# Half of the gate's columns of a hybrid decoder layer in seven products over all rows, in turn with the plain half

## The chip, the cores and the metric

One core of one Trainium2 chip runs the whole layer in one launch. The metric is the device time in microseconds of that launch; lower is better. TensorE is called PE, VectorE DVE, ScalarE ACT, GpSimd POOL and SyncE SP, as in the profile.

## The reference, cut to what matters

The layer has 256 rows (tokens) of 2048 values. After two token mixers and an MLP, each row passes a gated per-layer embedding, and that last line is what the change touches:

```python
x = x + merged @ w_out[i]
hm = rmsnorm(x, g_mlp[i])
x = x + jnp.square(jax.nn.relu(hm @ w_up[i])) @ w_down[i]
hp = rmsnorm(x, g_ple[i])
x = x + (p[i] @ w_ple_proj[i]) * jax.nn.sigmoid(hp @ w_ple_gate[i])
```

`w_ple_gate` is 2048 x 2048, all values are float32.

## The kernel before

Every product is made in three matmuls on split operands: an operand is cut into a high part (`wh`, a copy by ACT to a type that PE takes at full rate) and a remainder (`wl`, a subtraction by DVE). `split_weights` does that for 128x1024 pieces of a loaded quarter of weights (`raw`, 1 MB, three buffers; `wh` and `wl` have three buffers each). A matmul writes 128 rows by 512 columns into a bank of PSUM; there are eight banks, four under the name `ps_mm` and four under `ps_at`. Each engine works through its own list of instructions in a fixed order and waits in it for semaphores.

The MLP runs in blocks `s` of 1024 hidden columns. `up_units` makes the hidden values, transposed; `hidden` squares them and, for most blocks, also adds four sums of the 128x128 pieces of a pair of row tiles, so that `fast_units` can make a 2x2 product of blocks in seven products in place of eight. `plain_units` makes it in eight. `together` calls such streams in turn by fixed fractions. The row residual is `xr` (two tiles of 128 rows), to which `add_rows` adds.

The block `s = 7` is plain (`last_units`, 16 units), in turn with the embedding `p @ w_ple_proj` (`embedding_units`, into `em`). As column groups of 512 of `xr` are complete, `finished` sums their squares on ACT (`squares_rows`) and sets `turn` a few microseconds later by a clock that is counted in the program: PE transposes `xr` by 128x128 pieces, ACT and DVE split each pair of pieces into `h3`, scaled by the gain. `later(us, ...)` and `advance(us)` are that clock: they decide only where in the order an instruction stands.

The gate then runs over four groups of 512 columns. Each loads four quarters of weights, and 16 slices of 128 of the inner dimension go through three matmuls for each of the two row tiles: 384 matmuls. `gate_out` ends a group: sigmoid by ACT (with the row norm `rms[1]` as scale), product with `em` and addition of `xr` by DVE, and the store from SP. SP also issues all weight loads, in its own order.

Of the kernel before, what the change touches and what calls it, by code (L numbers as in the profile page):

```python
# [59 lines left out]
def layer_kernel(ctx: ExitStack, tc: tile.TileContext, xt, xm, pt, gains, qkg, cst,  # L60
# [15 lines left out]
    def bank(tag):  # L76
        return psum.tile([P, 512], F32, tag=tag, name=f"ps_{tag}")
# [415 lines left out]
    mw = mlp.enter_context(tc.tile_pool(name="mw", bufs=2))  # L493
    FAST = [(s, 0) for s in range(7)]

    def hidden(s, fast):

        n = 8 if fast else 4  # L500
        nc.scalar.activation(s, s, AF.Relu)
        r = mw.tile([P, n, P], F32, tag="hr", name="hr", bufs=1)
        nc.scalar.activation(r[:, 0:4, :].rearrange("p a t -> p (a t)"),
                             s.rearrange("p a t -> p (a t)"), AF.Square)
        if fast:
            a21, a11, a22, a12 = (r[:, i, :] for i in range(4))
            nc.vector.tensor_tensor(r[:, 4, :], a11, a21, op=ALU.subtract)
            nc.vector.tensor_tensor(r[:, 5, :], a21, a22, op=ALU.subtract)
            nc.vector.tensor_tensor(r[:, 6, :], r[:, 5, :], a11, op=ALU.subtract)
            nc.vector.tensor_tensor(r[:, 7, :], r[:, 6, :], a12, op=ALU.add)  # L510
        u = hid.tile([P, 2, n, P], F32R, tag="hid", name="u")
        split(u[:, 0], u[:, 1], r)
        return u
# [162 lines left out]
    ss2 = const.tile([P, 2, 4], F32, name="ss2")  # L676
    h3 = []

    def finished(g):
        if g == 0:  # L680
            h3.extend(new_acts("h3_", pool=blk))
        for tt in range(2):
            squares_rows(tt, g, ss2, mw.tile([P, PIECE], F32, tag="cp", name="junk", bufs=5))
        later(3, turn, g, h3, 2)

    def last_units(u):
        for n in range(2):
            yield from plain_units(7, n, u)
            finished(2 * n)
            finished(2 * n + 1)  # L690

    hids = [[]]
    for _ in up_units(0, hids[0]):
# [11 lines left out]
    later(6, lambda: rms.append(rows_norm(ss2, "rt2", mw)))  # L705


    def gate_out(g, tt, ps, c0, n):

        a, c = g * PIECE + c0, slice(g * PIECE + c0, g * PIECE + c0 + n)  # L710
        o = mw.tile([P, n], F32, tag="cp", name="o", bufs=5)
        nc.scalar.activation(o, ps[:, c0:c0 + n], AF.Sigmoid, scale=rms[1][:, tt:tt + 1])
# [4 lines left out]
    for g in range(4):  # L717
        ps = [bank("mm") if g % 2 else bank("at") for _ in range(2)]
        for c in range(4):
            for i, (wh, wl) in enumerate(weights(wpg[g, c], 4, PIECE)):  # L720
                kt = 4 * c + i
                for tt in range(2):
                    t = slice(tt * P, (tt + 1) * P)
                    nc.tensor.matmul(ps[tt], h3[kt][:, 0, t], wh, start=kt == 0, stop=False)  # L724
                    nc.tensor.matmul(ps[tt], h3[kt][:, 0, t], wl, start=False, stop=False)  # L725
                    nc.tensor.matmul(ps[tt], h3[kt][:, 1, t], wh, start=False, stop=kt == DT - 1)
                advance(1.36)
        for tt in range(2):
            gate_out(g, tt, ps[tt], 0, PIECE)
    mlp.close()  # L730


# [61 lines left out]
```

## Time and profile before

| | us |
|---|---|
| median of 3 runs | 1487.3 (1486.57 to 1488.2) |
| the profiled execution, whole | 1486.83 |
| its span in the trace | 1485.1 |
| last MLP block with the embedding, 1331.30 to 1389.88 | 58.58 |
| gate, 1389.88 to 1479.03 | 89.15 |
| end, 1479.03 to 1485.10 | 6.07 |

The stretches are cut at the first and last matmuls of a part. Matmuls overlap in the trace: each shows from its start to its modelled end, so their cost is read from start to start. The rows the prediction uses stand in a section of their own.

### The profile page before, as it was taken

To read this page: it belongs to the slowest core of one execution; us is meant where nothing else is said; L and a number is where in the kernel's file an instruction comes from. 1 tells how busy PE (TensorE), PEld (TensorE's weight loads), DVE (VectorE), ACT (ScalarE), POOL (GpSimd) and SP (SyncE) were. 2 spreads that over 40 slices of the span, in tenths; PEclk is the share of its full clock that TensorE was granted. 3 is DMA by queue.
4 is the path that set the end of the run, shared out by engine and by line. 5 is a ranking of instruction groups with operands and counts; after the bars stand their busy time and mean duration, and the time that the engine had idled before them with its cause. 6 is when DMAs were issued, how large, how long until landed. Compare 5 with 4: busy or idle time off the path is not lost.

```text
span 1485.1 us, 17838 instructions
## 1 busy us (share of the span) xinstructions
PE 1470.0 (99%) x6960; PEld 1209.4 (81%) x6960; DVE 1002.1 (67%) x1209; ACT 839.2 (57%) x1084; POOL 49.2 (3%) x65
## 2 busy tenths in 40 slices
PE   8999999999999999999999999999999999999998
PEld 6788888888888888888787887878888788888886
DVE  5975555455555555556878879788787878766654
ACT  6545555488834444546655655656565655656543
POOL 0641000000000000000000000000000000000000
PEclk9999999999999999999999999999999999999999
DMA  8555544544455555557455564645546465444563
GB/s 334 197 193 179 172 167 169 174 167 171 171 197 197 173 197 184 185 193 289 142 201 195 175 225 141 227 168 197 200 157 238 144 205 194 154 144 167 206 218 109
DMA packets 40341, 279.09 MB, mean 188 GB/s; under 512 B 4624, under 2 KB 4880, under 8 KB 7104
## 3 DMA queue, kind: packets, MB, share of 16 engines
q1 hardware_dynamic: 39600, 275.01, 53.4%
q0 software_dynamic: 512, 2.92, 0.5%
q8 instruction: 54, 0.88, 0.2%
q14 instruction: 31, 0.25, 0.0%
q10 hardware_dynamic: 144, 0.02, 0.0%
HBM read 275.83 MB, written 2.10 MB: 187 GB/s over the span
## 4 chain that ended last, share of the span: by engine, by line
PE 91%; DVE 4%; issue 2%; ACT 1%; DMA 1%; SPq 0%; DVEq 0%; ACTq 0%
PE ps_mm L525 15%; PE ps_mm L139 13%; PE ps_mm L138 13%; PE ps_mm L137 13%; PE ps_mm L526 8%; PE ps_mm L628 4%; PE ps_mm L629 4%; PE ps_mm L627 3%; PE ps_at L547 3%; PE ps_at L545 2%; PE ps_at L549 2%; DVE wl L83 2%; ACT wh L82 1%; PE ps_at L725 1%; PE ps_at L724 1%
## 5 line engine op out<-in xcount | busy, mean ns | idle before, releaser
L83 DVE TENSOR_TENSOR wl<-raw,wh 128x1024 fp32r<-128x1024 f32 (+1 forms) x462 | 563.9, 1229 | 336.4 <-ACT wh L82 330.6
L82 ACT ACTIVATE wh<-raw 128x1024 fp32r<-128x1024 f32 (+1 forms) x462 | 484.9, 1053 | 388.6 <-PE ps_mm L139 209.4
L525 PE MATMUL ps_mm<-h,wh 128*128 128x512 f32 x1024 | 366.0, 398 | 0.0
L526 PE MATMUL ps_mm<-h,wl 128*128 128x256 f32 x1024 | 287.2, 281 | 0.4
L137 PE MATMUL ps_mm<-wh,h 128*128 128x512 f32 x640 | 254.9, 399 | 2.0 <-ACT wh L82 1.7
L138 PE MATMUL ps_mm<-wl,h 128*128 128x512 f32 x640 | 250.9, 392 | 1.2 <-DVE wl L83 1.1
L139 PE MATMUL ps_mm<-wh,h 128*128 128x512 f32 x640 | 250.8, 392 | 0.0
L525 PEld LDWEIGHTS ps_mm<-h,wh 128*128 128x128 f32 x1024 | 192.3, 188 | 46.2 <-ACT wh L82 2.2
L526 PEld LDWEIGHTS ps_mm<-h,wl 128*128 128x128 f32 x1024 | 193.2, 189 | 8.1 <-DVE wl L83 3.1
L83 DVE TENSOR_TENSOR wl<-quart,wh 128x1024 fp32r<-128x1024 f32 x98 | 120.0, 1224 | 83.7 <-ACT wh L82 83.5
L82 ACT ACTIVATE wh<-quart 128x1024 fp32r<-128x1024 f32 x98 | 104.0, 1061 | 123.4 <-PE ps_mm L525 89.1
L138 PEld LDWEIGHTS ps_mm<-wl,h 128*128 128x128 f32 x640 | 120.9, 189 | 27.9 <-DVE wl L83 3.9
L137 PEld LDWEIGHTS ps_mm<-wh,h 128*128 128x128 f32 x640 | 120.6, 189 | 28.1 <-ACT wh L82 4.4
L139 PEld LDWEIGHTS ps_mm<-wh,h 128*128 128x128 f32 x640 | 120.7, 189 | 25.5
L628 PE MATMUL ps_mm<-wl,u 128*128 128x512 f32 x256 | 101.9, 398 | 4.0 <-DVE wl L83 3.9
L629 PE MATMUL ps_mm<-wh,u 128*128 128x512 f32 x256 | 100.2, 391 | 0.0
L627 PE MATMUL ps_mm<-wh,u 128*128 128x512 f32 x256 | 98.0, 392 | 0.0
L547 PE MATMUL ps_at<-wl,u 128*128 128x512 f32 x196 | 80.4, 410 | 0.0
L545 PE MATMUL ps_at<-wh,u 128*128 128x512 f32 x196 | 78.6, 401 | 0.0
L549 PE MATMUL ps_at<-wh,u 128*128 128x512 f32 x196 | 76.8, 392 | 0.0
L559 DVE TENSOR_TENSOR quart<-quart 128x2048 f32<-128x2048 f32 x28 | 64.0, 2287 | 0.5
L628 PEld LDWEIGHTS ps_mm<-wl,u 128*128 128x128 f32 x256 | 48.1, 188 | 18.3 <-DVE wl L83 9.3
(198 smaller groups left out, 1704.8 us busy)
## 6 DMA issues: line engine op xcount, KB each, us to landing
raw<-in_wa SPq DMA_DIRECT2D x79, 1024.0 KB, 4.8
raw<-in_wup SPq DMA_DIRECT2D x64, 1024.0 KB, 4.8
raw<-in_wdn SPq DMA_DIRECT2D x36, 1024.0 KB, 4.8
quart<-in_wdn SPq DMA_DIRECT2D x28, 1024.0 KB, 4.8
raw<-in_wo SPq DMA_DIRECT2D x16, 1024.0 KB, 4.8
raw<-in_wpg SPq DMA_DIRECT2D x16, 1024.0 KB, 4.8
raw<-in_wba SPq DMA_DIRECT2D x8, 1024.0 KB, 4.8
raw<-in_wbb SPq DMA_DIRECT2D x8, 1024.0 KB, 4.7
```

What stands on the lines that cost most here:

```text
L82: nc.scalar.activation(hi, src, AF.Copy)
L83: nc.vector.tensor_tensor(lo, src, hi.bitcast(F32), op=ALU.subtract)
L137: nc.tensor.matmul(ps[tt], lhs[kt][:, 0, t], wh, start=kt == 0, stop=False)
L138: nc.tensor.matmul(ps[tt], lhs[kt][:, 0, t], wl, start=False, stop=False)
L139: nc.tensor.matmul(ps[tt], lhs[kt][:, 1, t], wh, start=False, stop=kt == last)
L525: nc.tensor.matmul(ps, wh, flat(h2[kt]), start=kt == 0, stop=False)
L526: nc.tensor.matmul(ps[:, :T], wl, h2[kt][:, 0, :], start=False, stop=kt == DT - 1)
L545: nc.tensor.matmul(ps, f[k][:, 0, a, :], wh, start=start and k == 0, stop=False, skip_group_check=not start)
L547: nc.tensor.matmul(ps, f[k][:, 0, a, :], wl, start=False, stop=False, skip_group_check=not start)
L627: nc.tensor.matmul(ps[tt], u[k][:, 0, a, :], wh, start=i + k == 0, stop=False)
L628: nc.tensor.matmul(ps[tt], u[k][:, 0, a, :], wl, start=False, stop=False)
L629: nc.tensor.matmul(ps[tt], u[k][:, 1, a, :], wh, start=False, stop=last)
```

## The change

The left 1024 of the gate's 2048 output columns stay plain (`gate_plain`: two groups of 512, 16 units, 192 matmuls). The right 1024 are computed as a 2x2 product of blocks: rows in two tiles, inner dimension in two halves, columns in two groups of 512. `gate_fast` makes it in seven products of 24 matmuls (14 units, 168 matmuls). Sums of the weights are needed: `chain` is a buffer of two quarters into which further quarters are added by DMAs from POOL (`add_loaded`, 12 transfers of 512 KB); `right` is summed on DVE from two loads. The sums on the side of the rows are made by `four_sums`, so `x` is turned by pairs of tiles: PE transposes, ACT copies with the gain into the buffer `hr` (one buffer), DVE makes four sums, and one split of 128x1024 is written. Six pairs of eight are turned during the last MLP block (groups are now finished one by one), two in the gate. The products' results are kept by ACT and combined by DVE ahead of `gate_out`. Host code orders the weights by `halves`. The core of the diff:

```diff
+    def four_sums(r):
+        a21, a11, a22, a12 = (r[:, i, :] for i in range(4))
+        nc.vector.tensor_tensor(r[:, 4, :], a11, a21, op=ALU.subtract)
+        nc.vector.tensor_tensor(r[:, 5, :], a21, a22, op=ALU.subtract)
+        nc.vector.tensor_tensor(r[:, 6, :], r[:, 5, :], a11, op=ALU.subtract)
+        nc.vector.tensor_tensor(r[:, 7, :], r[:, 6, :], a12, op=ALU.add)
...
+    def turn_pair(k):
+        tp = bank("at")
+        for i in range(2):
+            for tt in range(2):
+                o = (2 * i + tt) * P
+                nc.tensor.transpose(tp[:, o:o + P],
+                                    xr[tt][:, (2 * k + i) * P:(2 * k + i + 1) * P], ident)
+        r = mw.tile([P, 8, P], F32, tag="hr", name="hr", bufs=1)
+        for i in range(2):
+            nc.scalar.activation(r[:, 2 * i:2 * i + 2, :].rearrange("p a t -> p (a t)"),
+                                 tp[:, i * T:(i + 1) * T], AF.Copy,
+                                 scale=gn[:, 2, 2 * k + i:2 * k + i + 1])
+        four_sums(r)
+        u = pair_tile(k)
+        split(u[:, 0], u[:, 1], r)
+        h3.append(u)
...
-        later(3, turn, g, h3, 2)
+        later(3, turn_pair, 2 * g)
+        later(4.5, turn_pair, 2 * g + 1)
...
+    def gate_fast():
...
+        def add_loaded(q, c, i, j):
+            for k in range(0, 4, 2):
+                nc.gpsimd.dma_start(q[:, k:k + 2, :].rearrange("p k c -> p (k c)"),
+                                    wpg[1, i, j, c, :, k * PIECE:(k + 2) * PIECE],
+                                    accum_op=ALU.add)
+
+        def product(ps, a, b, start, then=None):
+            for c in range(2):
+                for p0 in range(2):
+                    parts = split_weights(b(c)[:, 2 * p0:2 * p0 + 2, :], 2, PIECE)
...
+                if then:
+                    add_loaded(b(c), c, *then)
+                if c == 0:
+                    yield
...
+        def finish(tt, j, t, ps, op):
+            nc.vector.tensor_tensor(t, t, ps, op=op)
+            gate_out(tt, (2 + j) * PIECE, t)
...
+        chain = quarter(0, 0, room)
+        px, py = bank("at"), bank("at")
+        yield from product(px, A11, lambda c: chain[c], True, (0, 1))
+        keep_later("x", px)
+        yield
+        yield from product(py, A12, lambda c: load(wpg[1, 1, 0, c], 4, PIECE), True)
+        finish_later(0.6, 1, 0, "x", py, ALU.add)
+        yield
+        pz = bank("at")
+        yield from product(pz, S1, lambda c: chain[c], True, (1, 1))
...
+    together((0.9, 16, gate_plain()), (1.9, 14, gate_fast()))
```

The products follow as A11, A12, S1, S4, S2, S3, A22; `chain` is used by the first, third, fifth and seventh.

What stands in a row on the engines, first ACT at the beginning of the gate, before: `L85` are the copies of the turn, `L82` the high parts of weights and `L214` a step of the row norm. The brackets name the semaphores that an instruction waits for, by engine or DMA queue; numbers behind names are buffers.

```order
L214 ACTIVATE rs_11096<-rv_11094 128x2 [waits DVE_49]
L82 ACTIVATE wh_11084<-raw_11078 128x1024 [waits PE_49,Activation_49]
L85 ACTIVATE h3_2_10766<-ps_at_11036,gn_75 128x256 [waits PE_49]
L85 ACTIVATE h3_2_10766<-ps_at_11045,gn_75 128x256 [waits PE_49]
L85 ACTIVATE h3_2_10766<-ps_at_11036,gn_75 128x256 [waits DVE_49]
L85 ACTIVATE h3_2_10766<-ps_at_11045,gn_75 128x256 [waits DVE_49]
L82 ACTIVATE wh_11125<-raw_11123 128x1024 [waits DMAHW6_49,PE_49,Activation_49]
L85 ACTIVATE h3_3_10767<-ps_at_11054,gn_75 128x256 [waits PE_49]
L85 ACTIVATE h3_3_10767<-ps_at_11063,gn_75 128x256 [waits PE_49]
L85 ACTIVATE h3_3_10767<-ps_at_11054,gn_75 128x256 [waits DVE_49]
L85 ACTIVATE h3_3_10767<-ps_at_11063,gn_75 128x256 [waits DVE_49]
L82 ACTIVATE wh_11129<-raw_11123 128x1024 [waits PE_49,Activation_49]
```

And now, at the same place: `L700` are the copies of a pair into `hr`, `h3u` the split of a pair, `gq` is the weight buffer `chain`.

```order
L214 ACTIVATE rs_11137<-rv_11135 128x2 [waits DVE_49]
L700 ACTIVATE hr_11091<-ps_at_11086,gn_75 128x256 [waits PE_49,Activation_49]
L700 ACTIVATE hr_11091<-ps_at_11086,gn_75 128x256
L82 ACTIVATE h3u_11098<-hr_11091 128x1024 [waits DVE_49,Activation_49]
L700 ACTIVATE hr_11112<-ps_at_11107,gn_75 128x256 [waits DVE_49,PE_49]
L700 ACTIVATE hr_11112<-ps_at_11107,gn_75 128x256
L82 ACTIVATE h3u_11119<-hr_11112 128x1024 [waits DVE_49,Activation_49]
L82 ACTIVATE wh_11128<-gq_11122 128x1024 [waits DMAHW0_49]
L82 ACTIVATE wh_11149<-gq_11122 128x1024
L82 ACTIVATE wh_11163<-raw_11161 128x1024 [waits DMAHW5_49]
L82 ACTIVATE wh_11167<-raw_11161 128x1024 [waits DVE_49,PE_49]
```

The weight splits that stood between the copies of the turn have moved behind both pairs; the first is that of the first fast product.

Next, ACT around the first sigmoid of the gate, before:

```order
L82 ACTIVATE wh_11159<-raw_11157 128x1024 [waits DMAHW7_49,PE_49,Activation_49]
L82 ACTIVATE wh_11163<-raw_11157 128x1024 [waits PE_49,Activation_49]
L82 ACTIVATE wh_11205<-raw_11203 128x1024 [waits DMAHW0_49,DVE_49,PE_49]
L82 ACTIVATE wh_11209<-raw_11203 128x1024 [waits DVE_49,PE_49]
L712 ACT_TABLE_LOAD
L712 ACTIVATE o_11191<-ps_at_11006,rt2_11095 128x512 [waits PE_49]
L712 ACTIVATE o_11196<-ps_at_11007,rt2_11095 128x512 [waits PE_49]
L82 ACTIVATE wh_11239<-raw_11237 128x1024 [waits DMAHW1_49,DVE_49]
L82 ACTIVATE wh_11243<-raw_11237 128x1024 [waits DVE_49,PE_49]
```

And now: `gq` belongs to a fast product, `raw_11330` to the plain half.

```order
L82 ACTIVATE wh_11267<-raw_11265 128x1024 [waits DMAHW5_49,DVE_49,PE_49]
L82 ACTIVATE wh_11279<-raw_11277 128x1024 [waits DMAHW6_49,DVE_49,PE_49]
L82 ACTIVATE wh_11308<-gq_11122 128x1024 [waits DMASW5_49,DVE_49,PE_49]
L82 ACTIVATE wh_11318<-gq_11122 128x1024 [waits DMASW6_49,DVE_49,PE_49]
L743 ACT_TABLE_LOAD
L743 ACTIVATE o_11296<-gk_11211,rt2_11136 128x512 [waits DVE_49]
L82 ACTIVATE wh_11332<-raw_11330 128x1024 [waits DMAHW7_49,PE_49]
L82 ACTIVATE wh_11336<-raw_11330 128x1024 [waits PE_49,Activation_49]
L82 ACTIVATE wh_11352<-gq_11123 128x1024 [waits DMASW7_49,DVE_49,PE_49]
```

The table load and the sigmoid have moved from the border of two plain groups to a place between a fast product's pieces and the plain half's.

Last, the loads on SP at the beginning of the gate, before:

```order
L91 DMA raw_11008<-in_wpg 128x2048 [waits DMAHW2_49,DVE_49]
L91 DMA raw_11078<-in_wpg 128x2048 [waits DMAHW0_49,DVE_49]
L91 DMA raw_11123<-in_wpg 128x2048 [waits DMAHW3_49,DVE_49]
L91 DMA raw_11157<-in_wpg 128x2048 [waits DMAHW4_49,DVE_49]
L91 DMA raw_11203<-in_wpg 128x2048 [waits DMAHW5_49,DVE_49]
L91 DMA raw_11237<-in_wpg 128x2048 [waits DMAHW6_49,DVE_49]
L91 DMA raw_11271<-in_wpg 128x2048 [waits DMAHW7_49,DVE_49]
```

And now: `raw_11219`, `raw_11231`, `raw_11265` and `raw_11277` are the A12 product's.

```order
L91 DMA raw_11058<-in_wpg 128x2048 [waits DMAHW2_49,DVE_49]
L91 DMA raw_11161<-in_wpg 128x2048 [waits DMAHW0_49,DVE_49]
L91 DMA raw_11219<-in_wpg 128x2048 [waits DMAHW3_49,DVE_49]
L91 DMA raw_11231<-in_wpg 128x2048 [waits DMAHW4_49,DVE_49]
L780 DMA gq_11122<-in_wpg 128x2048 [waits PE_49]
L780 DMA gq_11123<-in_wpg 128x2048 [waits PE_49]
L780 DMA gq_11374<-in_wpg 128x2048 [waits PE_49]
L780 DMA gq_11375<-in_wpg 128x2048 [waits PE_49]
L91 DMA raw_11243<-in_wpg 128x2048 [waits DMAHW5_49,DVE_49]
L91 DMA raw_11265<-in_wpg 128x2048 [waits DMAHW6_49,DVE_49]
L91 DMA raw_11277<-in_wpg 128x2048 [waits DMAHW7_49,DVE_49]
L91 DMA raw_11330<-in_wpg 128x2048 [waits DMAHW4_49,DVE_49]
```

Four loads of `chain` and `right` have come in, and the product over A12, whose function of `c` loads, has four.

## Rows read from the trace of the kernel before

**Rows 1.** The page's part 1: busy time, share of the span, instructions.

```profile
PE 1470.0 (99%) x6960; PEld 1209.4 (81%) x6960; DVE 1002.1 (67%) x1209; ACT 839.2 (57%) x1084; POOL 49.2 (3%) x65
```

**Rows 2.** Stretches: length, busy (instructions) of PE, PEld, DVE, ACT, POOL; PEclk, DMA, GB/s.

```profile
1331.30:1389.88 58.58, 58.58 (x269) 48.44 (x267) 35.83 (x41) 35.71 (x54) 0.00 (x0) 1.00 0.54 189
1389.88:1479.03 89.15, 89.15 (x401) 73.46 (x399) 49.73 (x59) 42.18 (x51) 0.00 (x0) 1.00 0.50 171
```

**Rows 3.** Timeline of PE, end of the gate: start, duration, instruction.

```profile
1476.37 0.39 PE L725 MATMUL ps_mm<-wl,h 128*128 128x512 f32 x1
1476.60 0.39 PE L726 MATMUL ps_mm<-wh,h 128*128 128x512 f32 x1
...
1478.64 0.39 PE L726 MATMUL ps_mm<-wh,h 128*128 128x512 f32 x1
```

**Rows 4.** Timeline at a turn of x in the gate: transposes, copies, next matmul.

```profile
1393.97 1.04 PE L465 MATMUL ps_at<-idt,xr 128*128 128x128 f32 x8
...
1394.60 1.94 ACT L85 ACTIVATE h<-ps_at,gn 128x256 fp32r<-128x256 f32 x4 [0.66 <-PE ps_at L465]
...
1394.76 0.47 PE L724 MATMUL ps_at<-wh,h 128*128 128x512 f32 x1
```

**Rows 5.** Timelines of DVE and ACT, an MLP block's sums and split.

```profile
682.92 0.28 DVE L508 TENSOR_TENSOR hr<-hr 128x128 f32<-128x128 f32 x1
...
683.56 0.29 DVE L510 TENSOR_TENSOR hr<-hr 128x128 f32<-128x128 f32 x1
...
683.95 1.06 ACT L82 ACTIVATE u<-hr 128x1024 fp32r<-128x1024 f32 x1
...
685.05 1.22 DVE L83 TENSOR_TENSOR u<-hr,u 128x1024 fp32r<-128x1024 f32 x1
```

**Rows 6.** Groups by line: count, then busy us and mean ns, then idle before.

```profile
L82 ACT ACTIVATE wh<-raw 128x1024 fp32r<-128x1024 f32 x30 | 31.8, 1060 | 37.9 <-PE ps_mm L726 18.5 <-PE ps_at L726 17.8 <-PE ps_at L629 1.7
L83 DVE TENSOR_TENSOR wl<-raw,wh 128x1024 fp32r<-128x1024 f32 x30 | 36.6, 1224 | 31.3 <-ACT wh L82 31.1
L559 DVE TENSOR_TENSOR quart<-quart 128x2048 f32<-128x2048 f32 x28 | 64.0, 2287 | 0.5
L712 ACT ACTIVATE o<-ps_at,rt 128x512 f32<-128x512 f32 x4 | 2.6, 688 | 1.0 <-PE ps_at L726 1.0
L713 DVE TENSOR_TENSOR o<-o,em 128x512 f32<-128x512 f32 x8 | 5.4, 692 | 7.5 <-ACT o L712 7.5
```

**Rows 7.** Timeline of PE at the kernel's start, and one stretch (columns of Rows 2).

```profile
7.68 0.39 PE L139 MATMUL ps_mm<-wh,h 128*128 128x512 f32 x1
9.80 0.73 PE L137 MATMUL ps_mm<-wh,h 128*128 128x512 f32 x2 [1.73 <-ACT wh L82]
10.53 0.64 PE L138 MATMUL ps_mm<-wl,h 128*128 128x512 f32 x1
...
13.96 0.48 PE L138 MATMUL ps_mm<-wl,h 128*128 128x512 f32 x1
...
13.00:14.00 1.00, 1.00 (x4) 0.71 (x4) 1.00 (x3) 1.00 (x3) 0.00 (x0) 0.50 1.00 410
```

**Rows 8.** DMA issues: count, KB each, us to landing; one stretch near the start.

```profile
raw<-in_wpg SPq DMA_DIRECT2D x14, 1024.0 KB, 4.8
...
cs<-in_cst POOLq DMA_DIRECT2D x1, 608.0 KB, 6.6
...
20.00:30.00 10.00, 10.00 (x46) 8.28 (x45) 6.87 (x10) 7.43 (x15) 0.53 (x1) 1.00 1.02 424
```

**Rows 9.** Timeline of ACT at the gate's first sigmoid.

```profile
1412.14 1.28 ACT L712 ACT_TABLE_LOAD   x1
...
1414.60 1.05 ACT L82 ACTIVATE wh<-raw 128x1024 fp32r<-128x1024 f32 x1
```

**Rows 10.** PE's waits over the whole span: us, times, longest.

```profile
PE ps_mm L628 <- DVE wl L83: 3.9, 7, 1.2
```

**Rows 11.** Timeline of DVE, end of the kernel.

```profile
1480.39 1.28 DVE L714 TENSOR_TENSOR o<-o,xr 128x512 f32<-128x512 f32 x2
```

More of the change, by code (lines that the diff above doesn't have):

```diff
@@ L505, in hidden @@
         if fast:
[L506 to L510, printed above, removed]
+            four_sums(r)
         u = hid.tile([P, 2, n, P], F32R, tag="hid", name="u")
@@ L677, in layer_kernel, with pair_tile @@
     h3 = []
+    def pair_tile(k):
+        if k < 4:
+            return block([P, 2, 8, P], F32R, f"h3_{k}", blk)
+        if k < 6:
+            return mw.tile([P, 2, 8, P], F32R, tag="quart", name="h3q", bufs=4)
+        return hid.tile([P, 2, 8, P], F32R, tag="hid", name="h3u")
+    def turn_pair(k):
[10 more added lines that the diff above has]
+                                 scale=gn[:, 2, 2 * k + i:2 * k + i + 1])
+        four_sums(r)
+        u = pair_tile(k)
+        split(u[:, 0], u[:, 1], r)
+        h3.append(u)
     def finished(g):
-        if g == 0:
-            h3.extend(new_acts("h3_", pool=blk))
         for tt in range(2):
             squares_rows(tt, g, ss2, mw.tile([P, PIECE], F32, tag="cp", name="junk", bufs=5))
-        later(3, turn, g, h3, 2)
+        later(3, turn_pair, 2 * g)
+        later(4.5, turn_pair, 2 * g + 1)
     def last_units(u):
         for n in range(2):
-            yield from plain_units(7, n, u)
-            finished(2 * n)
-            finished(2 * n + 1)
+            units = plain_units(7, n, u)
+            for i in range(8):
+                next(units)
+                if i % 4 == 3:
+                    finished(2 * n + i // 4)
+                yield
     hids = [[]]
@@ L705, in layer_kernel, with gate_out @@
     later(6, lambda: rms.append(rows_norm(ss2, "rt2", mw)))
[L708 to L712, printed above, removed]
+    def gate_out(tt, c0, gate):
+        c = slice(c0, c0 + PIECE)
+        o = mw.tile([P, PIECE], F32, tag="cp", name="o", bufs=5)
+        nc.scalar.activation(o, gate, AF.Sigmoid, scale=rms[1][:, tt:tt + 1])
         nc.vector.tensor_tensor(o, o, em[tt][:, c], op=ALU.mult)
@@ L715, in gate_out, with gate_plain @@
         nc.sync.dma_start(out[tt, :, c], o)
[L717 to L721, printed above, removed]
-                for tt in range(2):
[L723 to L729, printed above, removed]
+    def gate_plain():
+        for j in range(2):
+            ps = [bank("mm") for _ in range(2)]
+            for c in range(2):
+                for i in range(2):
+                    raw = load(wpg[0, i, j, c], 4, PIECE)
+                    for k, (wh, wl) in enumerate(split_weights(raw, 4, PIECE)):
+                        for tt in range(2):
+                            a, u = 2 * i + tt, h3[4 * c + k]
+                            last = c == i == 1 and k == 3
+                            nc.tensor.matmul(ps[tt], u[:, 0, a, :], wh, start=c + i + k == 0,
+                                             stop=False)
+                            nc.tensor.matmul(ps[tt], u[:, 0, a, :], wl, start=False, stop=False)
+                            nc.tensor.matmul(ps[tt], u[:, 1, a, :], wh, start=False, stop=last)
+                        advance(1.36)
+                        if k == 1:
+                            yield
+                    if c + i < 2:
+                        yield
+            if j:
+                for tt in range(2):
+                    gate_out(tt, j * PIECE, ps[tt])
+            else:
+                for tt in range(2):
+                    later(0.6 + 1.5 * tt, gate_out, tt, j * PIECE, ps[tt])
+            yield
@@ L751, in quarters, with halves @@
     return np.ascontiguousarray(w).reshape(k // 1024, n // 1024, 2, 2, P, 4 * 512)
+def halves(w):
+    k, n = w.shape
+    w = w.reshape(k // 1024, 4, 2, P, n // 1024, 2, 512).transpose(4, 2, 5, 0, 3, 1, 6)
+    return np.ascontiguousarray(w).reshape(n // 1024, 2, 2, k // 1024, P, 4 * 512)
 def columns(a):
```

59 lines of the change are left out of this document (58 added, 1 removed).

## Prediction

> **What bounds the kernel now.** I read the page first: TensorE is busy for 99% of the span [rows 1], so what a change is worth is the number of matmul slots it saves, less the waits it makes. Then the stretches by time [rows 2]: in the last MLP block (58.58 us) and in the gate (89.15 us) PE is busy throughout at a granted clock of 1.00, while VectorE works 49.73 us of the gate's 89.15 and ScalarE 42.18. The slack on both is what the change spends. Then the order of time inside the gate. A 128x512 matmul shows 0.39 us, but its successor starts 0.23 us later (1476.37 to 1476.60; 1476.37 to the last at 1478.64 is ten steps, 0.227 each) [rows 3]. So one matmul costs 0.227 us of the path, not 0.39.
>
> The profiled execution took 1486.83 us around a span of 1485.1; the median of the runs is 1487.3. The sum below is made against 1486.83.
>
> **The change part by part.**
>
> *Matmuls.* The gate had 4 column groups x 16 x 2 x 3 = 384. Now the plain half has 192 and seven products of 8 x 3 have 168: 360 together, 24 fewer, as the program's order also has it. 24 x 0.227 = **-5.4 us**. The 32 transposes remain; 16 of them stood in the gate, 8 do now, the others move into the MLP block: nothing in the sum (eight cost 0.79 us, 1393.97 to 1394.76 [rows 4]).
>
> *The last two pairs of x.* This is the step that decides. In the old turn, four ScalarE copies and four VectorE subtractions ran side by side: the copies took 1.94 us and PE met no wait [rows 4]. Now one pair is a chain across both engines: two copies, four sums, a split on ScalarE, its remainder on VectorE. All go through one buffer, `hr`, so pair 7 may not copy until pair 6's remainder is written. The ScalarE order shown with the change has nothing between these steps, and behind them stands the first weight split of the first product, which PE needs after 24 gate matmuls.
>
> The chain's length: two copies 0.95 (half of 1.94). From the second sum's start to the last one's end 0.93, then the split 0.10 later, 1.06 long, and the remainder 0.04 after that, 1.22 long: all four steps stand in the trace for an MLP block (682.92 to 683.85, 683.95, 685.05) [rows 5]. With 0.05 at each change of engine, pair 6 takes 0.95 + 0.98 + 0.10 + 1.06 + 0.04 + 1.22 + 0.04 = 4.39. Pair 7 up to its split's end takes 3.09, and the weight split behind it 1.06, less 0.1 where two of an engine's instructions overlap. Sum 8.4. It starts when pair 6's transposes are there: 18 matmuls (4.08) and 0.63 after the transposes began (1393.97 to 1394.60 [rows 4]), at 4.7 us of the gate. So PE gets its first `wh` at 13.1, but is there at 24 x 0.227 + 0.79 = 6.2: it waits 6.9. The low part `wl` follows later, since VectorE finishes pair 7's remainder only at 13.4 and takes 1.22 [rows 6] more: another 1.2. **+8.1 us**. Below: if half of each latency were hidden, 7.5. Queued behind on ScalarE are all further splits, so nothing can run ahead.
>
> *TensorE's clock.* Early in the kernel PE sat idle from 8.07 to 9.80; the granted clock was 0.50 some microseconds later, which is the 1.2 of the two levels 1.2 and 2.4 GHz, and from 10.53 to 13.96 lie eight matmul starts, 0.43 us each [rows 7]. An idle of 6.9 us is longer, so I expect the same once: 3.4 us at half speed cost **+1.7**. Bounds 0 (no fall) and 3. [...]
>
> *Loads.* The A12 product calls for its weight quarter anew for each half of it, so that each quarter is fetched twice: 4 loads, where 2 would do (the SP order shown with the change). The raw pool has three buffers. The second two wait until a buffer is split, and then PE has 6 + 6 + 12 matmuls (5.4 us) less one ScalarE split (1.06) until it needs them: 4.4 us for a load that takes 4.8 [rows 8], while the GpSimd queue adds into SBUF beside it. Two such loads, and each late `wh` brings a late `wl`: **+1.5**, between 0 and 4. The bus moved 424 GB/s when asked [rows 8], and the gate runs at 171 [rows 2]; 24 MB in place of 16 still fit, so only landing times hurt. The Trainium skill (DMA: Bandwidth & Descriptors, section "Issuing engines are not separate DMA queues") says that transfers from all queues interleave on the same engines, so the adds would delay these loads; a landing of 1 MB behind 1 MB of adds would by it be the upper bound rather than the value taken.
>
> *The first sigmoid.* The table load (1.28) and the sigmoids stood ahead of a split that PE did not need at once: the load at 1412.14, the split at 1414.60, and no wait of PE [rows 9]. Now, between two products, ScalarE has a split for a 6-matmul piece, the table load, one sigmoid, and the split of the plain half. Its buffers let it start the first of these only after PE has left the third piece before: 1.06 + 1.28 + 0.69 + 1.06 = 4.1 against 18 matmuls, 4.1. VectorE must do two 0.69 us operations of the output [rows 6] before that split's remainder, so `wl` comes about **+1.2** late; bounds 0 and 1.7.
>
> *The remaining splits.* VectorE's account of the gate: 44 splits x 1.224 + 2 sums x 2.287 + 4 x 0.69 + 16 x 0.69 = 72 us of 82 [rows 6], with two of its instructions per 2.7 us of PE in the fast halves. In the MLP, which is as dense, a plain product sometimes waits for `wl`: 3.9 us in 7 places [rows 10]. I take **+0.8**, between 0 and 2.5. The turns of pairs 2 to 5 now stand before the embedding's `wl` in the MLP block: **+0.6**, between 0 and 1.6.
>
> *The end.* From the last matmul's end (1478.64 + 0.39) to the last addition's (1480.39 + 1.28) were 2.64 us [rows 3, 11]. Now follow an addition out of PSUM, the sigmoid, the product, the addition: 4 x 0.69 + latencies = 2.9, up to 1 us more while the plain half's last four VectorE operations are ahead: **+0.7** (0.3 to 1.4). The last store is the same.
>
> Sum: -5.4 + 8.1 + 1.7 + 1.5 + 1.2 + 0.8 + 0.6 + 0.7 = +9.2; 1486.83 + 9.2 = **1496**. With all terms at their low ends: -5.4 + 7.5 + 0 + 0 + 0 + 0 + 0 + 0.3 = +2.4, 1489; at the high ends -5.4 + 8.1 + 3 + 4 + 1.7 + 2.5 + 1.6 + 1.4 = +16.9, 1504.
>
> **The rivals.**
>
> *The turn is covered (faster).* Place: ScalarE between the first gate split and the first product. If pair 7's copies did not have to wait for pair 6's remainder, or if the first product's split were done ahead of both turns, the 8.1 would shrink; below a wait of about 2 us at that place the clock holds too, and the saving shows: 1486.83 - 5.4 + 0.7 and 0 to 2 for the rest, 1482 to 1484. For it: half of ScalarE's time in the gate is free [rows 2]. Against it: the order on an engine is fixed, and the single `hr` is in it.
>
> *The later waits are repaid (no change).* During the wait, the loads land and ScalarE gets ahead; the clock and the small terms come to nearly nothing, and the stall stays at its low end with them: 1486 to 1490. For it: the small terms are estimates of waits under 2 us. Against it: three split buffers let an engine be ahead by 2 splits only.
>
> *The adds arrive late (much slower).* Twelve transfers of 512 KB add weights onto `chain` in place. Between one use of a half and the next PE has 96 matmuls, 21.8 us; less two splits some 19 us stay for two transfers in a row, so it decides from about 9 us for each. The nearest row, a plain 608 KB transfer of the same queue on a full bus, took 6.6 us [rows 8]; in proportion 5.6. If reading the destination doubles it, 11: 2 x 2 us over, at three reuses, +12, 1508. The Trainium skill (DMA: Bandwidth & Descriptors, section "Rules for kernel authors") says that an accumulating transfer reads its destination and writes it later, which speaks for a doubling; no row here shows one.
>
> That fewer matmuls are not there is ruled out by the order.
>
> **How the numbers follow.** The forecast (1489 to 1504) gets 0.65; the adds late 0.14; covered 0.11; repaid 0.10. The likeliest case's time is 1496. From 1486 to 1508 are left out nearly all of "covered" and the upper half of "late", about 0.18. Both forecast and late adds are slower by over 0.2% (above 1490.3, about what this measurement can tell from no change), save a corner of the forecast that I give to chance: slower 0.78, same 0.11, faster 0.11.
>
> **What would show it.** In the trace of after: one PE wait of 6 to 8 us at the first matmul of the first product, released by ScalarE's `wh`, with ScalarE and VectorE taking turns on `hr` just before; right behind it a granted clock of 0.5 for about 3 us; a wait of one to three microseconds at the second half of A12, with ScalarE waiting for a DMA; matmuls 0.227 apart elsewhere. The prediction is wrong if that first wait is under 3 us, or if ScalarE waits for the GpSimd queue at the second and third use of `chain`.

## The result: 1% slower, and where the 16 us lie

| | us |
|---|---|
| before, 4 runs | 1486.93 (1485.55 to 1488.2) |
| after, 4 runs | 1502.89 (1502.53 to 1503.96) |
| ratio, with its 95% interval | 1.0112 (1.0097 to 1.0127) |
| profiled execution of after, its span | 1503.14, 1501.4 |

The changed kernel is 16 us slower. The forecast was 1496 with a range from 1486 to 1508: the sign and the range hold, the value is 7 us short.

The page of after has the fewer matmuls, 6936 for 6960 in [rows 1], and PE is still busy for 98% of the span. What is new is GpSimd's line, and the landing time of the gate's loads, which was 4.8 us in [rows 8]:

```profile
PE 1472.9 (98%) x6936; PEld 1207.4 (80%) x6936; DVE 1034.0 (69%) x1251; ACT 861.8 (57%) x1108; POOL 59.6 (4%) x77
...
L791 POOL DMA_DIRECT2D gq<-in_wpg x12 | 10.4, 872 | 1342.5 <-DVE wl L83 1342.5
...
raw<-in_wpg SPq DMA_DIRECT2D x14, 1024.0 KB, 6.2
```

The stretch of the gate in after (columns as in [rows 2]): 104.20 us where it was 89.15, and PE stands still for 12.6 of them. The DMA engines went from 0.50 to 0.77:

```profile
1390.90:1495.10 104.20, 91.59 (x369) 70.42 (x367) 73.10 (x81) 56.87 (x65) 10.44 (x12) 0.93 0.77 225
```

PE's timeline in after shows three places (start, duration, instruction, and in brackets the idle time and who ended it):

```profile
1396.82 0.60 PE L696 MATMUL ps_at<-idt,xr 128*128 128x128 f32 x4
1403.96 0.80 PE L802 MATMUL ps_at<-wh,h 128*128 128x512 f32 x1 [6.55 <-ACT wh L82]
1405.41 0.79 PE L804 MATMUL ps_at<-wl,h 128*128 128x512 f32 x1 [0.66 <-DVE wl L83]
...
1423.55 0.39 PE L761 MATMUL ps_mm<-wh,h3q 128*128 128x512 f32 x1
1426.87 0.79 PE L802 MATMUL ps_at<-wh,h3q 128*128 128x512 f32 x1 [2.93 <-ACT wh L82]
1428.13 0.79 PE L804 MATMUL ps_at<-wl,h3q 128*128 128x512 f32 x1 [0.47 <-DVE wl L83]
...
1440.86 0.50 PE L760 MATMUL ps_mm<-wl,h3q 128*128 128x512 f32 x1 [0.91 <-DVE wl L83]
```

The first is the first product, the second the second half of A12, the third the first sigmoid. Behind the first two the granted clock, the third number from the end, falls:

```profile
1400.00:1405.00 5.00, 0.80 (x1) 0.29 (x1) 3.17 (x6) 3.93 (x6) 0.00 (x0) 0.75 0.93 393
1405.00:1410.00 5.00, 4.59 (x12) 3.66 (x13) 3.59 (x4) 1.86 (x2) 1.81 (x2) 0.57 0.56 99
...
1425.00:1430.00 5.00, 2.66 (x5) 1.77 (x6) 2.02 (x2) 2.11 (x2) 0.00 (x0) 0.64 1.01 410
1430.00:1435.00 5.00, 5.00 (x17) 4.00 (x16) 1.65 (x2) 1.06 (x1) 0.86 (x1) 0.68 0.97 360
```

Inside them, in 1406 to 1408 us and in 1429 to 1432, it is 0.50, the lower of its two levels (1.2 and 2.4 GHz), and the matmuls start 0.43 us apart there.

ACT's timeline ahead of the first wait is the chain of the prediction, step by step: copies of pair 6, a wait for the sums, the split, a wait for the remainder of pair 6, the same for pair 7, and only then the first product's `wh` (its two pieces stand as one row):

```profile
1395.68 0.84 ACT L700 ACTIVATE hr<-ps_at,gn 128x256 f32<-128x256 f32 x2 [1.14 <-PE ps_at L696]
1397.59 1.06 ACT L82 ACTIVATE h3u<-hr 128x1024 fp32r<-128x1024 f32 x1 [1.07 <-DVE hr L501]
1400.00 0.84 ACT L700 ACTIVATE hr<-ps_at,gn 128x256 f32<-128x256 f32 x2 [1.35 <-DVE h3u L83]
1401.91 1.06 ACT L82 ACTIVATE h3u<-hr 128x1024 fp32r<-128x1024 f32 x1 [1.07 <-DVE hr L501]
1402.87 1.99 ACT L82 ACTIVATE wh<-gq 128x1024 fp32r<-128x1024 f32 x2
```

The second place is a load. ACT waited 4.88 us for A12's third load; the list of DMA issues of 1416 to 1419 us has that load (1 MB, 9.1 us to landing) and an adding transfer of GpSimd's queue beside it:

```profile
1425.76 1.06 ACT L82 ACTIVATE wh<-raw 128x1024 fp32r<-128x1024 f32 x1 [4.88 <-DMA raw<-in_wpg]
```

```profile
raw<-in_wpg SPq DMA_DIRECT2D x1, 1024.0 KB, 9.1
gq<-in_wpg POOLq DMA_DIRECT2D x1, 512.0 KB, 10.4
```

Start by start, every distance over the usual 0.227 taken together (less what the kernel before has of it), the terms of the prediction come out so:

| term | forecast | measured |
|---|---|---|
| 24 matmuls less | -5.4 | -5.4 (24 x 0.227) |
| first product waits for both turns | +8.1 | 6.7 + 1.2 = +7.9 |
| half clock | +1.7, once | 1.9 + 2.3 = +4.2, twice |
| A12's second half | +1.5 (0 to 4) | 3.1 + 1.0 = +4.1 |
| first sigmoid | +1.2 | 0.5 + 1.2 = +1.7 |
| other late splits (1452.39, 1455.93) | +0.8 | 0.35 + 0.87 = +1.2 |
| turns of pairs 2 to 5 | +0.6 | +0.2 |
| end | +0.7 | 6.70 - 6.46 = +0.2 |
| starts 0.23 to 0.24 apart, most of them in the products | none | about +2.2 |

The sum of the right column is 16.3, and so is the difference of the spans. The turns are read so: the gate begins 1.02 us later than before (1390.90 for 1389.88), and 0.79 of that are the eight transposes that moved into the MLP block, at their price of [rows 4].

### The profile page after: what moved, and what is told of

Read it like the earlier page. It is cut to its first block, busy times and chain, and to the rows that moved or that the text cites. A ratio compares the mean times of both kernels' runs of the same rounds, so it can differ in the third digit from the quotient of the medians.

```text
span 1501.4 us, 17919 instructions
## 1 busy us (share of the span) xinstructions
PE 1472.9 (98%) x6936; PEld 1207.4 (80%) x6936; DVE 1034.0 (69%) x1251; ACT 861.8 (57%) x1108; POOL 59.6 (4%) x77
## 4 chain that ended last, share of the span: by engine, by line
PE 90%; DVE 4%; issue 2%; DMA 2%; ACT 2%; SPq 0%; ACTq 0%; DVEq 0%
PE ps_mm L528 15%; PE ps_mm L139 13%; PE ps_mm L138 13%; PE ps_mm L137 13%; PE ps_mm L529 8%; PE ps_mm L631 4%; PE ps_mm L632 4%; PE ps_mm L630 3%; PE ps_at L550 3%; PE ps_at L548 2%; PE ps_at L552 2%; DVE wl L83 2%; ACT wh L82 1%; DMA raw<-in_wpg 1%; DMA raw<-in_wa 1%
## 5 line engine op out<-in xcount | busy, mean ns | idle before, releaser
L83 DVE TENSOR_TENSOR wl<-raw,wh 128x1024 fp32r<-128x1024 f32 (+1 forms) x454 | 554.1, 1229 | 304.1 <-ACT wh L82 297.7
L82 ACT ACTIVATE wh<-raw 128x1024 fp32r<-128x1024 f32 (+1 forms) x454 | 476.3, 1053 | 359.4 <-PE ps_mm L139 209.2
L82 ACT ACTIVATE wh<-quart 128x1024 fp32r<-128x1024 f32 x98 | 104.0, 1061 | 123.5 <-PE ps_mm L528 89.8
L791 POOL DMA_DIRECT2D gq<-in_wpg x12 | 10.4, 872 | 1342.5 <-DVE wl L83 1342.5
```

The lines of the kernel that those rows point to most:

```text
L82: nc.scalar.activation(hi, src, AF.Copy)
L83: nc.vector.tensor_tensor(lo, src, hi.bitcast(F32), op=ALU.subtract)
```

## Experiments

The theories at this point: **(T)** the first wait is the order on ACT, both turns ahead of the product's first split; **(L)** the second is the doubled load; **(D)** the second is the DMA engines' load, the adds above all. Each run below is compared with the kernel before on the same chip; its median was 1485.8 to 1486.6 there.

| kernel | us | ratio to before (95%) |
|---|---|---|
| turns earlier and apart | 1490.67 | 1.0033 (1.0020 to 1.0046) |
| A12 loaded once | 1500.86 | 1.0099 (1.0084 to 1.0114) |
| no adds | 1494.08 | 1.0055 (1.0040 to 1.0070) |
| own `hr` for pair 7 | 1502.50 | 1.0110 (1.0093 to 1.0127) |
| PE kept busy in both waits | 1500.57 | 1.0096 (1.0081 to 1.0112) |
| new turn, old gate | 1486.70 | 1.0006 (0.9998 to 1.0015) |
| turns apart and A12 loaded once | 1490.81 | 1.0034 (1.0022 to 1.0047) |
| the same, sums by GpSimd | 1493.01 | 1.0042 (1.0030 to 1.0055) |
| plain transfers for the adds | 1498.59 | 1.0078 (1.0063 to 1.0094) |
| turns apart, loaded once, no adds | 1484.24 | 0.9988 (0.9979 to 0.9997) |
| products first, loads earlier | 1485.38 | 0.9995 (0.9986 to 1.0004) |
| the same, a plain piece last | 1484.89 | 0.9990 (0.9981 to 0.9999) |

### The first wait: order, buffer or chain

**The new turn alone**, with the gate of the kernel before. Its product loop only takes its left operand from the pair tiles:

```diff
-                    nc.tensor.matmul(ps[tt], h3[kt][:, 0, t], wh, ...)
+                    u, a = h3[kt // 2], 2 * (kt % 2) + tt
+                    nc.tensor.matmul(ps[tt], u[:, 0, a, :], wh, ...)
```

> The new turn by pairs (two copies, four sums, split and remainder through one hr) with the gate of the kernel before, all 384 plain matmuls. If the turn's chain of itself stops TensorE, as the sum of the prediction has it that counted its length alone: the third weight split comes late, 6 to 8 us and a half clock: 1487 + 8 = 1495. If it is only the place of the chain (here the splits of the plain weights stand between its steps on ScalarE, in the changed kernel the first product's stands behind both): no wait over 1 us, 1487 to 1488.

Measured 1486.7, no difference, and no wait of PE in the gate. ACT's timeline of this run shows why: the splits of the plain weights (`wh<-raw`) stand between the steps of the turn.

```profile
1394.79 0.84 ACT L700 ACTIVATE hr<-ps_at,gn 128x256 f32<-128x256 f32 x2 [0.66 <-PE ps_at L696]
1396.13 1.06 ACT L82 ACTIVATE wh<-raw 128x1024 fp32r<-128x1024 f32 x1 [0.50 <-PE ps_at L757]
1397.10 1.04 ACT L82 ACTIVATE h3u<-hr 128x1024 fp32r<-128x1024 f32 x1
1399.31 1.06 ACT L82 ACTIVATE wh<-raw 128x1024 fp32r<-128x1024 f32 x1 [1.17 <-PE ps_at L757]
1400.28 0.82 ACT L700 ACTIVATE hr<-ps_at,gn 128x256 f32<-128x256 f32 x2
```

The chain itself costs nothing: it is its place.

**A buffer of its own for pair 7** takes away only the wait of 1.35 us that stands in ACT's rows above.

```diff
-        r = mw.tile([P, 8, P], F32, tag="hr", name="hr", bufs=1)
+        r = (hid.tile([P, 8, P], F32, tag="hid", name="hr7") if k == 7 else
+             mw.tile([P, 8, P], F32, tag="hr", name="hr", bufs=1))
```

> Pair 7 gets a work buffer of its own, so that its copies need not wait for pair 6's remainder; nothing else is moved. The rival of the prediction (the single buffer hr holds the chain up): the first wait falls from 6.55 to under 2 us, the clock holds: 1503 - 6.5 = about 1496. Theory (the place on ScalarE holds it up, with or without the buffer): ScalarE saves the 1.35 us that it waited for pair 6's remainder, less a part that the sums then wait for VectorE, the first wait is 5.2 to 5.9: 1501.5 to 1502.5.

The wait went from 6.55 to 5.70, as the theory had it; the 0.4 us in the time are within the noise. The single `hr` is not what holds the product up: with it gone, ACT waits 1.68 us for the sums.

```profile
1403.78 0.80 PE L803 MATMUL ps_at<-wh,h 128*128 128x512 f32 x1 [5.70 <-ACT wh L82]
```

**Turns earlier and apart.** The code sets the turns of the last column group at other times, with its squares and the norm behind them, and asks for the chain's first quarter ahead of the gate:

```diff
-        later(3, turn_pair, 2 * g)
-        later(4.5, turn_pair, 2 * g + 1)
+        later(1.5 if g == 3 else 3, turn_pair, 2 * g)
+        later(5.5 if g == 3 else 4.5, turn_pair, 2 * g + 1)
...
-        chain = quarter(0, 0, room)
```

> The last two pairs of x are turned earlier, and apart: pair 6 at 1.5 us after the last addition to x instead of 3, pair 7 at 5.5 instead of 4.5, so that weight splits stand between them on ScalarE, and the chain's first weights are asked for ahead of the gate. Theory (the first product's split is late because both turns stand in front of it on ScalarE): TensorE's first wait in the gate, 6.55 + 0.66 us in the profile of after, falls to about 1, and the half clock behind it, about 1.9 us, does not come: 1503 - 6.2 - 1.9 = about 1495. Rival (the wait is repaid: whoever reaches the later pieces earlier waits there): the second wait, at the second half of A12, grows by what the first one loses, and only 1 to 3 us are gained: 1500 to 1502.

1490.67: 12 us less than after, more than the 8.1 that the theory gave. The wait at the first product is gone altogether, since both of its first splits (`wh<-gq`) now stand ahead of pair 6's copies on ACT:

```profile
1391.40 1.06 ACT L82 ACTIVATE wh<-gq 128x1024 fp32r<-128x1024 f32 x1 [0.71 <-PE ps_at L632]
...
1394.18 1.06 ACT L82 ACTIVATE wh<-gq 128x1024 fp32r<-128x1024 f32 x1
1395.15 0.82 ACT L700 ACTIVATE hr<-ps_at,gn 128x256 f32<-128x256 f32 x2
```

With its half clock that place is worth 9.8 us from start to start; the rest came back in small parts behind it. One wait remains at A12's second half, 3.66 us, with half clock behind it, and one of 1.01 later:

```profile
1418.31 0.80 PE L805 MATMUL ps_at<-wh,h3q 128*128 128x512 f32 x1 [3.66 <-ACT wh L82]
1418.90 0.63 PE L763 MATMUL ps_mm<-wl,h3u 128*128 128x512 f32 x1
```

The rival (the time is given back at later waits) falls: the second wait grew by 0.7 us only. Theory T stands, shown from both sides: the chain costs nothing where splits stand between its steps, and the wait goes when the first product's splits no longer stand behind the chain. Which of the moves of this run (turns earlier, turns apart, the norm later, the load earlier) is needed was not tried.

### The second wait: the doubled load, or the DMA engines

**A12's quarters loaded once.**

```diff
-        yield from product(py, A12, lambda c: load(wpg[1, 1, 0, c], 4, PIECE), True)
+        once = {}
+        yield from product(py, A12, lambda c: once[c] if c in once else
+                           once.setdefault(c, load(wpg[1, 1, 0, c], 4, PIECE)), True)
```

> Each quarter of A12's weights is loaded once for both of its pieces, two loads of 1 MB less. Theory (the doubled load is the cause of the second wait: the third load must wait for a raw buffer): no wait at the second half of A12, 2.93 + 0.47 us and some 0.7 of uneven starts, and no half clock behind it, 2.3: 1503 - 6.4 = 1496.5. Rival (the wait only moves, since a raw buffer is now held over two pieces and the next plain load gets one later): the waits behind it, 1.6 us in the profile of after, grow by 2 to 4 us: 1499 to 1501.

1500.86: the rival's value, at best 2 us less, with an interval that overlaps that of after. PE no longer waits at A12's second half, but some ten microseconds later it waits 1.01 us for a `wh` and 3.92 for a `wl`. DVE's row of the same stretch says for what: a sum of the last quarter (L124, 2.29 us) had stood for 2.51 us until S4's load landed, with that `wl` queued behind it.

```profile
1438.83 0.79 PE L760 MATMUL ps_mm<-wl,h3q 128*128 128x512 f32 x1 [3.92 <-DVE wl L83]
```

```profile
1434.75 2.29 DVE L124 TENSOR_TENSOR gq<-gq,raw 128x2048 f32<-128x2048 f32 x1 [2.51 <-DMA raw<-in_wpg]
```

So the doubled load was only the first of the late ones. Theory L does not hold by itself.

**No adds.** The line that issues the adding transfers is left out.

```diff
-                if then:
-                    add_loaded(b(c), c, *then)
```

> The twelve adding transfers of GpSimd's queue are left out, so S1, S2 and A22 multiply weights that are not the right ones; every load of SyncE's queue, the doubled ones too, and every split stays. If the adds are what makes A12's third load late (it took 9.1 us to land beside them, against 4.8 in the kernel before): it lands in about 5, the second wait of 2.93 us shrinks to 0.5 or less and the half clock behind it, 2.3, does not come: 1503 - 4.8 = about 1498. If the doubled load alone is the cause and the adds cost nothing: the landing stays above 8 us and the time within 1 us of 1503. The first wait, 6.55 us, stays in both.

1494.08, 8.8 us less, though every doubled load stays: theory D. The expectation had 4.8; it had not counted the late `wl` of the second place nor the later splits, which went too. The waits behind the first product shrink to those at the sigmoid. The stretch of 1404 to 1428 us (first after, then this run) shows how much of the DMA engines the adds had taken, and the loads issued in 1414 to 1420 land in 4.8:

```profile
1404.00:1428.00 24.00, 20.08 (x73) 14.97 (x73) 13.35 (x12) 10.77 (x11) 3.54 (x4) 0.86 0.90 250
```

```profile
1404.00:1428.00 24.00, 24.00 (x97) 19.32 (x98) 15.10 (x14) 12.56 (x14) 0.00 (x0) 0.93 0.62 223
```

```profile
raw<-in_wpg SPq DMA_DIRECT2D x2, 1024.0 KB, 4.8
```

**Plain transfers in the place of the adds** tell the bytes from the adding.

```diff
                                     wpg[1, i, j, c, :, k * PIECE:(k + 2) * PIECE],
-                                    accum_op=ALU.add)
```

> The changed kernel with its twelve adding transfers made plain ones: the same bytes on the same queue into the same buffers at the same places, but they overwrite and do not add, so three products multiply weights that are not the right ones. Without these transfers the kernel took 1494.1 us, with them 1502.9. If it is the adding that fills the DMA engines (they were busy 0.90 of 1404 to 1428 us at 250 GB/s with the adds, and 0.62 at 223 GB/s without any): the third load of A12 lands in 5 to 6 us, the second wait is under 1 us, and the time is within 2 us of the run without: 1494 to 1496. If the 6.3 MB themselves are too much beside the other loads: 1500 or more, and the landing stays above 8 us.

1498.59, between the two answers: about half of the 8.8 us is the adding, and about half the bytes. By the times it is 4.3 and 4.5, by the ratios to the kernel before 5.1 and 3.4, so the halves are known to some 2 us only. A12's third load landed in 7.3 us, and ACT waited 3.01 us for it. The list of DMA queues of the gate (packets, MB, share of 16 engines; after, then this run) shows the same 6.29 MB at 30.2% and at 16.6%: adding costs a DMA engine 1.8 times the time.

```profile
q0 software_dynamic: 1728, 6.29, 30.2%
```

```profile
q0 software_dynamic: 1728, 6.29, 16.6%
```

### The clock

**PE kept busy.** 26 matmuls that nobody reads fill the first wait, 14 the second.

```diff
+        def warm(ps, n):
+            for _ in range(n):
+                nc.tensor.matmul(ps, h3[0][:, 0, 0, :], flat(h3[0][:, 0, 0:4, :]),
+                                 start=True, stop=True)
         px, py = bank("at"), bank("at")
+        warm(px, 26)
```

> 26 matmuls of 128x512 that nobody reads are put ahead of the first product (26 x 0.227 = 5.9 us, less than the wait of 6.55 + 0.66), and 14 ahead of the second half of A12 (3.2 us; the waits there are 2.93 + 0.47), each into a bank that the next product starts anew; all else stays. If idle time of TensorE is what brings the half clock: the granted clock stays 1.00 behind both places, the first matmul of the products starts when it did, and 1.9 + 2.3 us are gained: 1503 - 4.2 = about 1499. If the 0.43 us between starts there have another cause (weights arriving late for each matmul): no gain, 1503, or up to 0.5 more where the idle matmuls outlast the waits.

1500.57, 2.3 us less, which the intervals hardly tell from nothing; the rows do show what happened. At the second place the clock stayed at 1.00, where after had 0.64. At the first it fell all the same: two short waits were left there, 0.64 and 0.95 us with one matmul between them.

```profile
1397.72 6.16 PE L814 MATMUL ps_at<-h 128*128 128x512 f32 x26
1404.53 0.50 PE L802 MATMUL ps_at<-wh,h 128*128 128x512 f32 x1 [0.64 <-ACT wh L82]
1405.98 0.50 PE L804 MATMUL ps_at<-wl,h 128*128 128x512 f32 x1 [0.95 <-DVE wl L83]
```

Two stretches of this run, behind the first place and around the second:

```profile
1407.00:1408.00 1.00, 1.00 (x4) 0.75 (x3) 1.00 (x2) 0.00 (x0) 1.00 (x2) 0.50 0.00 0
...
1425.00:1430.00 5.00, 4.32 (x18) 2.96 (x17) 1.52 (x2) 2.24 (x3) 0.00 (x0) 1.00 1.04 421
```

So idle time brings the fall, shown at one place of the two, and part of what was gained there went into a wait of 1.92 us later, for a load. The Trainium skill (TensorE: Matmul & The Clock Gate, section "HAM oscillation — how this bites in real kernels") tells of a kernel whose waits for loads are each long enough to bring PE back to the lower clock, and in which this is paid at every one of them. After's two falls agree that it is paid more than once; the prediction counted one.

### Towards a version that beats both

**Both mends**, turns apart and A12 loaded once:

> The changed kernel with the turns earlier and apart, the chain's first weights asked for ahead of the gate, and A12's quarters loaded once. If the three causes found in its trace are all there is (19.2 us of late starts in the gate, of which 3 to 4 stay: splits late by up to 1 us, the table load): 1503 - 15.5 = 1487.5, no slower than the kernel before, at best 1485. If the saved matmuls bring the products so close that VectorE and ScalarE cannot keep up (44 splits, 72 us of VectorE in 82): 1490 or more, with many waits of 0.3 to 1 us for the low parts.

1490.81, no better than the turns alone (1490.67). The wait moved from A12 to DVE's sum: PE waited 3.02 us for a `wl` behind a sum that had waited 4.12 for its load. The 1487.5 of the expectation was a miss. The rows of this wait name the load, and not the length of DVE's or ACT's work; the next run tests it:

```profile
1439.37 0.50 PE L763 MATMUL ps_mm<-wl,h 128*128 128x512 f32 x1 [3.02 <-DVE wl L83]
```

```profile
1435.88 2.29 DVE L124 TENSOR_TENSOR gq<-gq,raw 128x2048 f32<-128x2048 f32 x1 [4.12 <-DMA raw<-in_wpg]
```

**The same without the adds:**

> The run with all three mends (1490.8 us; turns earlier and apart, chain asked for early, A12 loaded once), and the twelve adding transfers left out, so that three products multiply weights that are not the right ones; the splits, sums and matmuls all stay. Its trace had 8.4 us of late starts left, 3.3 + 1.4 + 1.0 of them with half clock of 1.4 behind, the largest where VectorE waited for a load. If what is left is the DMA engines' load (they were busy without a pause from 1404 to 1428 us): the big wait and the half clock go, 2 to 3 us of late starts stay, 1490.8 - 5.5 = 1485, or down to 1484, under the kernel before. If it is VectorE's and ScalarE's work: 1489 or more.

1484.24, 0.1% under the kernel before: PE waits 0.8 us in the whole gate. With turns and loads mended, the adds are nearly all of the waits that are left, by 6.6 us.

**The sums by GpSimd**, so that DVE need not stand in them:

```diff
-            later(2.5, nc.vector.tensor_tensor, right[c], right[c], b11[c], ALU.add)
+            later(2.5, nc.gpsimd.tensor_tensor, right[c], right[c], b11[c], ALU.add)
```

> The run with all three mends (turns earlier and apart, chain asked for early, A12 loaded once; 1490.8 us), and besides the two sums of 128x2048 that VectorE makes for the last quarter (2.29 us each) are made by GpSimd. In the run before, VectorE stood in such a sum for 4.1 us until the load of its second operand landed, and the low part that TensorE needed was queued behind it: TensorE waited 3.0 us, with half clock behind it. If that queueing is what is left: 1490.8 - 3.0 - 1.4 - up to 1 = 1485.5 to 1486.5, level with the kernel before. If GpSimd's sums take VectorE's time in turn, or come too late for S3: 1488 or more.

1493.01, no better: 2 us more, with intervals that overlap. GpSimd takes 5.35 us for a sum, and DVE hardly moves meanwhile: two splits in 6.50 us that take 2.45 alone, one product of 128x512 in 5.09 that takes 0.69 in [rows 6].

```profile
1427.42 5.35 POOL L124 TENSOR_TENSOR gq<-gq,raw 128x2048 f32<-128x2048 f32 x1 [6.32 <-PE ps_at L808]
...
1433.87 5.58 POOL L124 TENSOR_TENSOR gq<-gq,raw 128x2048 f32<-128x2048 f32 x1
```

```profile
1428.49 6.50 DVE L83 TENSOR_TENSOR wl<-raw,wh 128x1024 fp32r<-128x1024 f32 x2 [0.18 <-ACT wh L82]
1434.91 5.09 DVE L747 TENSOR_TENSOR o<-o,em 128x512 f32<-128x512 f32 x1
```

**Products first, loads earlier.** A12's second quarter and S4's first go into free buffers of `hid`, so that the three `raw` buffers do not hold the loads back, and the products run half a piece ahead of the plain half:

```diff
+                if c:
+                    once[c] = room()
+                    nc.sync.dma_start(once[c].rearrange("p k c -> p (k c)"), wpg[1, 1, 0, c])
...
-    together((0.9, 16, gate_plain()), (1.9, 14, gate_fast()))
+    together((1.3, 16, gate_plain()), (0.9, 14, gate_fast()))
```

> As the run with all three mends (1490.8 us), with the products half a piece ahead of the plain half and not behind it, pair 7 turned at 6.5 us, A12's second quarter and S4's first one loaded into free buffers of the pool hid, so that the loads come earlier, and the plain half's first outputs 1.4 us later. If the loads that come late can be had earlier in this way, the waits of 3.3 and 1.4 us and the half clock go and the plain half ends last, with the shorter tail: 1490.8 - 5 to - 6 = 1485 to 1486, level with the kernel before or just under it. If the DMA engines are full in any order: 1489 to 1491.

1485.38, 17.5 us under after and level with before. The stretches of this run are the ones to read beside those of after: the DMA engines are busy without a pause (1.03 and 0.99), and PE is busy throughout. That it is the earlier loads which do this is argued, not shown: the order of the two halves, pair 7's turn and the plain half's outputs were moved with them.

```profile
1404.00:1428.00 24.00, 23.94 (x102) 18.02 (x101) 20.73 (x19) 16.36 (x18) 3.46 (x4) 1.00 1.03 335
1428.00:1452.00 24.00, 23.86 (x104) 18.77 (x103) 19.21 (x18) 14.79 (x16) 2.92 (x4) 1.00 0.99 261
```

**A plain piece last**, with the last product's second half one place earlier in the row of pieces:

```diff
+        if last:
+            at = len(due) - 1 - due[::-1].index(1)
+            due.insert(at - last, due.pop(at))
```

> As the run with the products ahead of the plain half (1485.4 us, 1.2 under the kernel before, which its interval does not tell from nothing), with the last piece of the last product put one plain piece earlier, so that its output is finished while TensorE still has two plain pieces to do. In that run 7.15 us lay between the last matmul's start and the end of the span, against 6.46 in the kernel before, since three outputs met on VectorE. If that is the cause of the longer tail: about 6.4, 0.7 gained, 1484.7, 0.1% under the kernel before. If the tail is that of the plain outputs alone and the earlier product only waits for its weights: 1485.4 or up to 1 more.

1484.89, 0.1% under the kernel before, with an interval that only just leaves out no change (0.9981 to 0.9999): a gain of this size is hardly told from none. From the last matmul's start to the end of the span are 6.4 us, as expected:

```profile
1477.50 0.39 PE L768 MATMUL ps_mm<-wh,h3u 128*128 128x512 f32 x1
```

Its gate has no wait of PE at all. Of the 5.4 us that 24 matmuls are worth, 1 is left. The starts in its gate come 3.5 us later in sum than 0.227 for a matmul and 0.1 for a transpose would give (in the kernel before 0.2), and the gate begins 1.8 us later, of which the eight moved transposes are 0.8. Why a product's matmuls start 0.231 apart and not 0.227 was not tried; without the adds they do too (0.230 to 0.232).

## Why the prediction was right, and where it was short

- **What bounds the kernel, and the matmuls (-5.4).** Right: what was saved and what was lost is read in PE's starts alone.
- **The last two pairs (+8.1; 7.9 measured).** The chain came step by step as added up: the wait for the product's first `wh` was forecast as 6.9, and is 6.55, or 6.7 from start to start; the late `wl` as 1.2, and is 1.2. What the step said on its cause was half right. Its sentence that all further splits are queued behind on ScalarE is the cause. The single `hr`, which it put ahead of that and which the rival "the turn is covered" makes one of its two conditions, is worth 0.85 us of the wait. The rival's other condition, the first split ahead of the turns, is the mend that worked.
- **The clock (+1.7; 4.2).** The step had the price of one fall right (1.9) and the count wrong: a wait of one to three microseconds at A12's second half stands among its signs, and it was 2.93, but no fall behind it was priced, and that one cost 2.3.
- **The loads (+1.5; 4.1).** This is the term that failed, with the second fall in its train. It counted 4.4 us of time against a landing of 4.8, and left the adds out of that landing, on the ground that 24 MB in place of 16 still fit under 424 GB/s. In the trace the load took 9.1 us. The bytes alone do not fill the engines: an adding transfer takes 1.8 times the time of a plain one, and over 24 us the engines were busy 0.90 at 250 GB/s. But they count too: with plain transfers in place of the adds the load still took 7.3 us and the kernel some 4 us more than without any. The sentence that the adds delay these loads was right, and its worth should have been in the value: taking the adds out gained 8.8 us, the half clock and the later waits included.
- **The rival "the adds arrive late" (0.14).** Wrong in its place, right in its agent: the first product that reuses a half never waited for an add (no engine's wait names GpSimd's queue), and 512 KB landed in 7.0 us in the median, below the 9 from which it decides, though one took 10.4. What the adds delayed were the other loads.
- **The first sigmoid, the later splits, the turns, the end.** 1.7, 1.2, 0.2 and 0.2 for 1.2, 0.8, 0.6 and 0.7: within their bounds, the first at its upper one, save the end, which is just under its 0.3. Left out were the uneven starts, about 2.2 us, against the sign that matmuls elsewhere would start 0.227 apart.
- **The range.** It held in part by luck. The clock lies outside its bounds (4.2; 0 to 3), the loads at the edge of theirs (4.1; 0 to 4), and the uneven starts had no term; the sum stays under the 1504 of all high ends because the later splits, the turns and the end stayed well below theirs.
- **"The later waits are repaid".** Did not hold for the first wait (12 us came back when it went), but held among the loads: loading once, and filling both waits, gained less than the waits that they removed, since the next load was late in turn.

## What to carry to other kernels

A transfer that adds into memory is to be counted as nearly two in the DMA engines' time, and the question is not whether the bytes fit on the average but which load stands beside it in the few microseconds that it has. Where one engine turns an operand and splits weights, the order in its queue cost more here than the length of the chain: put the splits that the next products need ahead of the chain or between its steps. A load that is made twice, or late, was not mended alone here; look at which one is late next before you count the gain.

## What the runs showed of the hardware

- An accumulating transfer of 512 KB keeps the DMA engines busy 1.8 times as long as a plain one (30.2% for 16.6% of the same stretch, 6.29 MB each), and GpSimd's instruction that issues it takes 0.86 us in place of 0.53.
- A sum of 128x2048 float32 takes GpSimd 5.35 to 5.58 us and VectorE 2.29, and VectorE hardly moves meanwhile: an operation of 0.69 us that began during such a sum took 5.09 and ended 0.55 us after it (1440.00 for 1439.45). The Trainium skill (GPSIMD Engine Reference, section "8. Key points") says that the two share their interfaces to the buffer and contend where VectorE reads two inputs from it; the rows agree, and VectorE's subtraction and product both do.
- With PE kept busy, the granted clock fell to 0.50 behind two waits of 0.64 and 0.95 us with a single matmul between them, after six microseconds without a gap. It did not behind 0.30 and 0.91 us, with two matmuls between, at the sigmoid of after (1.00 in 1440 to 1445 us). What makes the difference was not tried.
